# A start-up reorder, a contiguous sum of squares and a 64-byte shift of the stationary weights in a one-core encoder layer

## The chip, the cores and the metric

The kernel runs on one core of one Trainium2 chip. The metric is the device time of one execution in microseconds (us); the value before is the median of three runs. Engines are named as in the profile: PE is the matrix engine's multiplications and PEld its loading of stationary operands, DVE the vector engine, ACT the scalar engine, POOL the GpSimd engine, SP the engine that issues the transfers.

## The reference

One layer of a bidirectional encoder over 256 tokens of width 2048, all in float32:

```python
h = rmsnorm(x, norm_pre_mix)
u = h @ w_in                     # 2048 x 10240, cut into q, f_fwd, f_bwd, v, g
# 16 heads of 128: gated linear recurrence in both directions, summed over directions
o = rmsnorm(recurrence(silu(q), gates(f_fwd), gates(f_bwd), v), g_norm) * silu(g)
x = x + rmsnorm(o @ w_out, norm_post_mix)
h = rmsnorm(x, norm_pre_ffn)
gate, val = split(dwconv3(h @ ffn_w_in))     # 2048 x 11264
x = x + rmsnorm((silu(gate) * val) @ ffn_w_out, norm_post_ffn)   # 5632 x 2048
```

The root mean square of `x` is not divided out ahead of the first product. The kernel multiplies the unnormalised `x` (times the norm's weights) into `w_in` and scales the results by `rs1`, one number for each token, so that the first products need not wait for the sum of squares.

## The kernel before, in words

**Precision.** Float32 products are made of float32r parts. Every operand `a` is split into `hi` (ACT's rounded copy) and `lo = a - hi` (DVE). A product is then three products: hi with hi, hi with lo, lo with hi.

**Weights.** Each weight matrix is laid out in chunks of 512 output columns. A chunk is read in 1 MB transfers of `[128, 4, 512]` into one of three buffers `raw` (rows of 8192 bytes in each of the 128 partitions). `load(pieces)` can cut such a transfer into pieces, which makes the rows shorter in proportion. `prep` splits each half of a `raw` (a "sub", two steps `k` of 128 along the sum) into `hi` and `lo` in one of four buffers `wsp`: a cast on ACT (line 136) and a subtraction on DVE (line 137). The very first sub is split in two halves, so that its first half can be used early. `LOOK = 3` subs are prepared ahead; in the first chunk it is one.

**Two kinds of product.** `gemm` (lines 181, 184, 185) keeps activations stationary and streams 512 weight columns: three matmuls of 512 columns for each `k` and each of two token tiles. It serves the chunks of `v`, `g`, `w_out`, the first chunk of `ffn_w_in` and `ffn_w_out`. `gemm_t` (lines 221, 223) turns the product around: the weights are stationary (128 columns of `wsp`, called `w` in the code) and the activations are streamed. For each of 4 column tiles `n` and each `k` it makes a long matmul (`hi` stationary, activations `hi` and `lo` together, 512 columns, line 221) and a short one (`lo` stationary, activations `hi`, 256 columns, line 223). It serves the 12 chunks of `q`, `f` and `b` and 21 of the 22 chunks of `ffn_w_in`. A chunk of 16 steps `k` has 64 such pairs. In each sub all 8 long and all 8 short ones are run together, and a counter `turn` swaps which kind goes first from one sub to the next; in the last sub of a chunk the groups are two long, two short.

**Where the weights lie.** For chunks that `gemm_t` uses ("turned"), `hi` and `lo` lie a little into their buffers:

```python
at0 = [1088 * i + (OFF[i] if turned else 0) for i in range(2)]
```

`OFF` counts float32 elements. The stationary weights and the streamed activations then have addresses that differ by 4 x 48 = 192 bytes modulo 256. For `gemm` there is no such shift: streamed weights and stationary activations differ by a multiple of 256 bytes.

**The start.** SP issues the first transfers in the order of the code: parameters, two `k` of `x` (transposed, `xs`, `load_x`), two quarters of the first weights, two more `k` of `x`, the other two quarters, and so on. Meanwhile PE does 24 transposes of an identity (line 284). `split_x` makes `hi` (ACT, line 302) and `lo` (DVE, line 305) of two `k` of `x`, one call ahead of each sub of the first chunk.

**The sum of squares.** While the second chunk is multiplied, one step of a list (`soon`) is emitted after each sub: four steps `square_x` (ACT squares four `k` of `xs` in place, line 313; DVE sums them over `k` with a reduction whose innermost step runs across `k`, line 314) and a step `mean_x` (a last reduction, line 317; a matmul with a column of ones, line 320; the square root on POOL, line 230). Two steps later `spread` turns `rs1` into a row `r1` for all partitions.

**Order.** The program is built with `schedule_with_timeline_sim=True`: a planner with a model of the engines decides each engine's order, except where `keep_in_program_order` holds an instruction. Engines then run their own lists in that order and wait for each other by semaphores.

Of the kernel before, what the change touches and what calls it, by code (L numbers as in the profile page):

```python
# [11 lines left out]
F32 = mybir.dt.float32  # L12
# [3 lines left out]
ALU = mybir.AluOpType  # L16
AX = mybir.AxisListType

P = 128
T = 256  # L20
# [8 lines left out]
EPS = 1e-6  # L29
NLEV = 7  # L30
LOOK = 3
OFF = (48, 48)
WARM = 24

ORDER = [(s, g) for g in range(NG - 1) for s in "qfbgv"][:-1]
# [12 lines left out]
def encoder_layer(  # L48
# [13 lines left out]
    nc = tc.nc  # L62
    V, S, G = nc.vector, nc.scalar, nc.gpsimd

    def pool(stack, name, bufs=1, **kw):
        return stack.enter_context(tc.tile_pool(name=name, bufs=bufs, **kw))
# [10 lines left out]
    def stile(n, name):  # L77
        return small.tile([P, n], F32, name=name, tag=name)
# [24 lines left out]
    soon, later, extra = deque(), deque(), []  # L103

    def step():
        if soon or later:
            (soon or later).popleft()()

    def load(pieces=1):
        ci, s = subs[at["load"]]  # L110
        wd, c, _ = chunks[ci]
        raw = wraw.tile([P, 4, 512], F32, name="raw", tag="raw")
        src = wd[c, s // 2].rearrange("p (k n) -> p k n", n=512)
        w = 4 // pieces
        raws[ci, s // 2] = raw
        at["load"] += 2
        for i in range(pieces):
            nc.sync.dma_start(raw[:, w * i : w * i + w], src[:, w * i : w * i + w])
            yield

    def prep(upto):
        while at["prep"] < min(upto, len(subs)):
            i = at["prep"]
            if at["load"] <= i:
                list(load())
            ci, s = subs[i]
            src = raws[ci, s // 2][:, 2 * (s % 2) : 2 * (s % 2) + 2, :]
            pl, sfx = (extra[0], str(s)) if ci == C_UP - 1 and s >= 2 * chunks[ci][2] - 4 else (wspl, "")


            w = pl.tile([P, 2 * 1088], F32R, name="wsp", tag="wsp" + sfx)
            turned = ci < len(ORDER) and ORDER[ci][0] in "qfb" or C_UP < ci < C_UP + 2 * NJ
            at0 = [1088 * i + (OFF[i] if turned else 0) for i in range(2)]
            hi, lo = (w[:, o : o + 1024].rearrange("p (j n) -> p j n", n=512) for o in at0)
            for j in [slice(0, 1), slice(1, 2)] if i == 0 else [slice(0, 2)]:
                S.copy(hi[:, j], src[:, j])  # L136
                V.tensor_tensor(lo[:, j], src[:, j], hi[:, j].bitcast(F32), op=ALU.subtract)  # L137
            parts[ci, s] = (hi, lo)
            at["prep"] += 1
# [3 lines left out]
    def flush():  # L143
        while soon or later:
            step()
# [46 lines left out]
    def gemm_t(xx, need=None, pre=None):  # L192


        ci = at["chunk"]
        at["chunk"] += 1
        nsub = 2 * chunks[ci][2]
        base = subs.index((ci, 0))
        ps = [ps_g.tile([P, 2, T], F32, name="pg", tag="pg") for _ in range(4)]
        turn = [0]  # L200
        for s in range(nsub):
            if s == need:
                flush()
            prep(base + s + (LOOK if ci else 1))
            if pre:
                pre(s)
            hi, lo = parts[ci, s]

            tiles = [(n, 2 * s + j) for n in range(4) for j in range(2)]
            if ci == s == 0:
                tiles.sort(key=lambda nk: nk[1])
            for run in [tiles] if s < nsub - 1 else [tiles[i : i + 2] for i in range(0, 8, 2)]:
                long = turn[0] % 2 == 0
                for kind in (long, not long):
                    for n, k in run:
                        w = (hi if kind else lo)[:, k % 2, n * P : (n + 1) * P]
                        stop = s == nsub - 1 and kind != long and k == 2 * nsub - 1
                        if kind:  # L220
                            nc.tensor.matmul(ps[n], w, xx[:, k], start=(k == 0), stop=stop)  # L221
                        else:
                            nc.tensor.matmul(ps[n][:, 0, :], w, xx[:, k, 0, :], start=False, stop=stop)  # L223
                turn[0] += 1
            step()
        return ps

    def rsqrt_mean(dst, ss, n):
        V.tensor_scalar(dst, ss, 1.0 / n, EPS, op0=ALU.mult, op1=ALU.add)
        G.tensor_tensor(dst, dst, mneg[:, : dst.shape[1]], op=ALU.pow)  # L230

    def spread(rs, name):

        tp = ps_t.tile([P, 2, T], F32, name="tp", tag="tp")
        for m in range(2):
            a = rs[:, m : m + 1].broadcast_to([P, P])
            nc.tensor.matmul(tp[:, 0, m * P : (m + 1) * P], a, ident, start=True, stop=True)
        S.copy(name, tp[:, 0, :])
# [20 lines left out]
    spool = pool(sstack, "start", side="right")  # L259
    xs = spool.tile([P, KT, T], F32, name="xs")  # L260

    def load_x(a, b):
        nc.sync.dma_start(xs[:, a:b], xt_v[:, a:b])

    nc.sync.dma_start(prm[:, :C_CW], par[:, :C_CW])
    load_x(0, 2)
    first = load(4)
    next(first), next(first)
    load_x(2, 4)
    list(first)  # L270
    load_x(4, 8)
    list(load(2))
    load_x(8, 12)
    load_x(12, 16)
    make_identity(nc, ident)
    G.memset(mneg, -0.5)

# [22 lines left out]
    def split_x(k2):  # L300
        for k in (2 * k2, 2 * k2 + 1):
            S.activation(xx[:, k, 0, :], xs[:, k, :], AF.Copy, scale=prm[:, C_PRE + k : C_PRE + k + 1])
        for k in (2 * k2, 2 * k2 + 1):
            w1, hi = prm[:, C_PRE + k : C_PRE + k + 1], xx[:, k, 0, :].bitcast(F32)
            V.scalar_tensor_tensor(xx[:, k, 1, :], xs[:, k, :], w1, hi, op0=ALU.mult, op1=ALU.subtract)

    ss1, rs1 = spool.tile([P, 5, T], F32, name="ss1"), stile(2, "rs1")
    one = spool.tile([P, 1], F32, name="one")
    G.memset(one, 1.0)

    def square_x(q):
        k = slice(4 * q, 4 * q + 4)
        tc.keep_in_program_order(S.activation(xs[:, k], xs[:, k], AF.Square))
        V.tensor_reduce(ss1[:, q, :], xs[:, k].rearrange("p k t -> p t k"), axis=AX.X, op=ALU.add)

    def mean_x():
        V.tensor_reduce(ss1[:, 4, :], ss1[:, :4].rearrange("p q t -> p t q"), axis=AX.X, op=ALU.add)
        tp = ps_t.tile([P, 2, T], F32, name="tp", tag="tp")
        for m in range(2):
            nc.tensor.matmul(tp[:, 0, m : m + 1], ss1[:, 4, m * P : (m + 1) * P], one, start=True, stop=True)  # L320
        rsqrt_mean(rs1, tp[:, 0, :2], D)
        soon.extend([nop, lambda: spread(rs1, r1)])

    split_x(0)
    ps0 = gemm_t(xx, pre=lambda s: split_x(s + 1) if 2 * s + 2 < KT else None)
    soon.extend([lambda q=q: square_x(q) for q in range(4)] + [mean_x])
    ps1 = gemm_t(xx)
    load_rest()
    sstack.close()
# [28 lines left out]
    def do_q(g):  # L358
        ps = gemm_t(xx) if g else ps0
        qT = hp.tile([P, HG, T], F32, name="qT", tag="qT")  # L360
        each_token(ps, qT, r1)
        sg = nat.tile([P, HG, T], F32, name="qn", tag="qn")
        S.activation(sg, qT, AF.Sigmoid)
        V.tensor_tensor(qT, qT, sg, op=ALU.mult)
        st["q", g] = qT
# [419 lines left out]
```

## Time and profile before

| | |
|---|---|
| median of three runs | 1356.26 us (1356.21 to 1358.15) |
| profiled execution, its own time | 1357.99 us |
| span of its instructions | 1356.1 us |
| granted clock of the matrix engine, mean | 0.997 |
| PE busy | 1343.2 us, 99% |
| PEld busy | 1160.6 us, 86% |
| DVE busy | 956.4 us, 71% |
| ACT busy | 697.6 us, 51% |
| moved by the transfers | 248.90 MB, mean 184 GB/s |

The span runs from the first to the last instruction; the profiled execution's own time is 1.9 us longer, for what lies around it. An engine's busy time includes overlapped, modelled ends of pipelined matmuls, so the spacing of matmuls is better read from starts than from durations. The chain of waits lists, in order of time, the work that ended last and what released it.

### The profile page before, as it was taken

To read this page: it belongs to the slowest core of one execution; us is meant where nothing else is said; L and a number is where in the kernel's file an instruction comes from. 1 tells how busy PE (TensorE), PEld (TensorE's weight loads), DVE (VectorE), ACT (ScalarE), POOL (GpSimd) and SP (SyncE) were. 2 spreads that over 40 slices of the span, in tenths; PEclk is the share of its full clock that TensorE was granted. 3 is DMA by queue.
4 is the path that set the end of the run, shared out by engine and by line. 5 is a ranking of instruction groups with operands and counts; after the bars stand their busy time and mean duration, and the time that the engine had idled before them with its cause. 6 is when DMAs were issued, how large, how long until landed. Compare 5 with 4: busy or idle time off the path is not lost.

```text
span 1356.1 us, 18012 instructions
## 1 busy us (share of the span) xinstructions
PE 1343.2 (99%) x7244; PEld 1160.6 (86%) x7244; DVE 956.4 (71%) x1208; ACT 697.6 (51%) x964; POOL 12.5 (1%) x22
## 2 busy tenths in 40 slices
PE   8999999999999999999999999999999999999997
PEld 7888988898898888888888888888888888888886
DVE  6898768866996887567767777777768674444444
ACT  6555545455545545457655555555556554434342
POOL 0000000000000000000000000000000000000000
PEclk9999999999999999999999999999999999999999
DMA  8454445435444534673455555555555556555552
GB/s 307 167 186 168 145 172 181 163 135 187 174 142 167 190 135 156 248 254 115 169 208 186 187 189 187 200 186 201 186 187 187 189 187 240 191 186 191 202 197 93
DMA packets 36356, 248.90 MB, mean 184 GB/s; under 512 B 4144, under 2 KB 4400, under 8 KB 6832
## 3 DMA queue, kind: packets, MB, share of 16 engines
q1 hardware_dynamic: 36272, 247.75, 52.0%
q8 instruction: 57, 0.93, 0.3%
q14 instruction: 27, 0.22, 0.1%
HBM read 245.63 MB, written 2.10 MB: 183 GB/s over the span
## 4 chain that ended last, share of the span: by engine, by line
PE 97%; DVE 1%; DMA 0%; issue 0%; ACT 0%; SPq 0%; DVEq 0%; POOLq 0%; POOL 0%; ACTq 0%
PE pg L221 35%; PE pg L223 18%; PE pg L181 13%; PE pg L184 13%; PE pg L185 13%; PE sc L468 3%; PE sc L434 1%; PE sc L525 1%; PE sc L493 1%; PE sc L524 1%; DMA raw<-in_w_in 0%; DVE wsp L137 0%; PE tp L248 0%; PE tp L620 0%; ACT wsp L136 0%
## 5 line engine op out<-in xcount | busy, mean ns | idle before, releaser
L137 DVE TENSOR_TENSOR wsp<-raw,wsp 128x1024 fp32r<-128x1024 f32 (+1 forms) x457 | 555.0, 1221 | 337.8 <-ACT wsp L136 335.5
L136 ACT CAST wsp<-raw 128x1024 fp32r<-128x1024 f32 (+1 forms) x457 | 478.4, 1049 | 519.1 <-PE pg L185 224.8
L221 PE MATMUL pg<-hh,wsp 128*128 128x512 f32 x1344 | 332.2, 392 | 0.0
L221 PEld LDWEIGHTS pg<-hh,wsp 128*128 128x128 f32 x1344 | 241.9, 188 | 44.1
L221 PE MATMUL pg<-xx,wsp 128*128 128x512 f32 x768 | 195.3, 397 | 0.3 <-DVE qn L355 0.3
L223 PEld LDWEIGHTS pg<-hh,wsp 128*128 128x128 f32 x1344 | 177.5, 188 | 12.1
L223 PE MATMUL pg<-hh,wsp 128*128 128x256 f32 x1344 | 180.8, 278 | 0.0
L221 PEld LDWEIGHTS pg<-xx,wsp 128*128 128x128 f32 x768 | 139.0, 190 | 25.9 <-issue 0.7
L184 PE MATMUL pg<-wsp,gg 128*128 128x512 f32 x352 | 136.9, 389 | 0.0
L185 PE MATMUL pg<-wsp,gg 128*128 128x512 f32 x352 | 136.9, 389 | 0.0
L181 PE MATMUL pg<-wsp,gg 128*128 128x512 f32 x352 | 136.8, 389 | 0.0
L223 PEld LDWEIGHTS pg<-xx,wsp 128*128 128x128 f32 x768 | 103.4, 188 | 10.8 <-DVE wsp L137 3.4
L223 PE MATMUL pg<-xx,wsp 128*128 128x256 f32 x768 | 108.4, 280 | 3.0 <-DVE wsp L137 3.0
L184 PE MATMUL pg<-wsp,xx 128*128 128x512 f32 x256 | 100.1, 391 | 0.0
L185 PE MATMUL pg<-wsp,xx 128*128 128x512 f32 x256 | 100.0, 391 | 0.0
L181 PE MATMUL pg<-wsp,xx 128*128 128x512 f32 x256 | 97.2, 390 | 0.0
L185 PEld LDWEIGHTS pg<-wsp,gg 128*128 128x128 f32 x352 | 66.1, 188 | 13.8
L181 PEld LDWEIGHTS pg<-wsp,gg 128*128 128x128 f32 x352 | 66.1, 188 | 13.7
L184 PEld LDWEIGHTS pg<-wsp,gg 128*128 128x128 f32 x352 | 66.1, 188 | 13.6
L184 PEld LDWEIGHTS pg<-wsp,xx 128*128 128x128 f32 x256 | 48.1, 188 | 9.8
L181 PEld LDWEIGHTS pg<-wsp,xx 128*128 128x128 f32 x256 | 48.1, 188 | 9.8
L185 PEld LDWEIGHTS pg<-wsp,xx 128*128 128x128 f32 x256 | 48.1, 188 | 9.7
(137 smaller groups left out, 1178.0 us busy)
## 6 DMA issues: line engine op xcount, KB each, us to landing
raw<-in_w_up SPq DMA_DIRECT2D x88, 1024.0 KB, 4.9
raw<-in_w_in SPq DMA_DIRECT2D x78, 1024.0 KB, 4.9
raw<-in_w_dn SPq DMA_DIRECT2D x44, 1024.0 KB, 4.9
raw<-in_w_o SPq DMA_DIRECT2D x16, 1024.0 KB, 4.9
x<-in_x SPq DMA_DIRECT2D x1, 2048.0 KB, 7.7
wp<-in_post SPq DMA_DIRECT2D x2, 1024.0 KB, 6.2
out<-fw SPq DMA_DIRECT2D x8, 256.0 KB, 2.7
xs<-in_xt SPq DMA_DIRECT2D x3, 512.0 KB, 9.5
```

What stands on the lines that cost most here:

```text
L136: S.copy(hi[:, j], src[:, j])
L137: V.tensor_tensor(lo[:, j], src[:, j], hi[:, j].bitcast(F32), op=ALU.subtract)
L181: mm = nc.tensor.matmul(ps[m], a, hi[:, j, :], start=(k == 0), stop=False)
L184: nc.tensor.matmul(ps[m], a, lo[:, j, :], start=False, stop=False)
L185: nc.tensor.matmul(ps[m], b, hi[:, j, :], start=False, stop=(k == 2 * nsub - 1))
L221: nc.tensor.matmul(ps[n], w, xx[:, k], start=(k == 0), stop=stop)
L223: nc.tensor.matmul(ps[n][:, 0, :], w, xx[:, k, 0, :], start=False, stop=stop)
L434: nc.tensor.matmul(o, ones, a[:, i * 512 : i * 512 + 512], start=(j == 0), stop=(j == 1))
L468: nc.tensor.matmul(sc[:, j, :], kc[0][:, h, sl], r, start=True, stop=True)
L493: nc.tensor.matmul(sc[:, h, :], ks[:, d, h, s0 : s0 + P], qs[:, 1 - d, h, t0 : t0 + P], start=True, stop=True)
L524: nc.tensor.matmul(o[:, h, :], Sd[:, 2 * h + b, :], v[:, b, cs], start=True, stop=False)
L525: nc.tensor.matmul(o[:, h, :], So[1 - b][:, h, :], v[:, 1 - b, cs], start=False, stop=True)
```

## The change

Five edits in one:

1. `OFF` goes from 48 to 32 elements for both halves: stationary weights lie 128 in place of 192 bytes off the activations modulo 256.
2. In the first chunk the counter `turn` stays at zero, so that every sub there runs its long matmuls first.
3. The first 1 MB of weights comes in two pieces in place of four (rows of 4096 in place of 2048 bytes), the second 1 MB in one piece in place of two (8192 in place of 4096), the last half of `x` in one transfer in place of two (8192 in place of 4096).
4. The squares of `x` are summed by contiguous additions in place of reductions: three additions of 1024 elements in each partition, then one of 512 and one of 256.
5. The squares are done in two steps of `soon` in place of four, so `mean_x` comes two steps earlier.

```diff
-OFF = (48, 48)
+OFF = (32, 32)
...
-                turn[0] += 1
+                turn[0] += ci > 0
...
     nc.sync.dma_start(prm[:, :C_CW], par[:, :C_CW])
     load_x(0, 2)
-    first = load(4)
-    next(first), next(first)
+    first = load(2)
+    next(first)
     load_x(2, 4)
     list(first)
     load_x(4, 8)
-    list(load(2))
-    load_x(8, 12)
-    load_x(12, 16)
+    list(load())
+    load_x(8, 16)
...
-    ss1, rs1 = spool.tile([P, 5, T], F32, name="ss1"), stile(2, "rs1")
+    rs1 = stile(2, "rs1")
...
         tc.keep_in_program_order(S.activation(xs[:, k], xs[:, k], AF.Square))
-        V.tensor_reduce(ss1[:, q, :], xs[:, k].rearrange("p k t -> p t k"), axis=AX.X, op=ALU.add)
+        if q:
+            V.tensor_tensor(xs[:, :4], xs[:, :4], xs[:, k], op=ALU.add)

     def mean_x():
-        V.tensor_reduce(ss1[:, 4, :], ss1[:, :4].rearrange("p q t -> p t q"), axis=AX.X, op=ALU.add)
+        for n in (2, 1):
+            V.tensor_tensor(xs[:, :n], xs[:, :n], xs[:, n : 2 * n], op=ALU.add)
         tp = ps_t.tile([P, 2, T], F32, name="tp", tag="tp")
         for m in range(2):
-            nc.tensor.matmul(tp[:, 0, m : m + 1], ss1[:, 4, m * P : (m + 1) * P], one, start=True, stop=True)
+            nc.tensor.matmul(tp[:, 0, m : m + 1], xs[:, 0, m * P : (m + 1) * P], one, start=True, stop=True)
...
-    soon.extend([lambda q=q: square_x(q) for q in range(4)] + [mean_x])
+    soon.extend([lambda q=q: (square_x(q), square_x(q + 1)) for q in (0, 2)] + [mean_x])
```

## The prediction

> **What bounds the kernel now.** I read the page first: busy times and the chain that ended last.
>
> ```profile
> span 1356.1 us, 18012 instructions
> PE 1343.2 (99%) x7244; PEld 1160.6 (86%) x7244; DVE 956.4 (71%) x1208; ACT 697.6 (51%) x964; POOL 12.5 (1%) x22
> ...
> PE 97%; DVE 1%; DMA 0%; issue 0%; ACT 0%; SPq 0%; DVEq 0%; POOLq 0%; POOL 0%; ACTq 0%
> PE pg L221 35%; PE pg L223 18%; PE pg L181 13%; PE pg L184 13%; PE pg L185 13%; PE sc L468 3%; PE sc L434 1%; PE sc L525 1%; PE sc L493 1%; PE sc L524 1%; DMA raw<-in_w_in 0%; DVE wsp L137 0%; PE tp L248 0%; PE tp L620 0%; ACT wsp L136 0%
> ```
>
> PE carries 97% of the chain, so there are only two ways to move the time: shorten PE's few waits (3% of 1356 us hold them all, the tail at the end included), or change the spacing of the matmuls themselves. The turned products, lines 221 and 223, are 53% of the chain, the only ones whose addresses change.
>
> Then the spacing. First the chain inside one chunk of turned products (start, length, what; "x16" is 16 matmuls in a row), then the chain of the plain product (lines 181, 184, 185 in turn), last the durations (min/median/max in ns) of both kinds.
>
> ```profile
> 717.39 1.89 PE pg L223 x16
> 719.28 3.67 PE pg L221 x16
> ...
> 728.51 1.13 PE pg L223 x10
> ...
> 731.03 0.93 PE pg L221 x4
> ```
>
> ```profile
> 1109.95 0.23 PE pg L181
> ...
> 1126.27 0.23 PE pg L181
> ```
>
> ```profile
> L181 PE MATMUL pg<-wsp,gg x339: 389/389/389, 1109.8 to 1339.6; 128*128 128x512 f32 x170
> ...
> L221 PE MATMUL pg<-hh,wsp x1246: 388/392/397, 659.8 to 1090.0; 128*128 128x512 f32 x178
> ...
> L223 PE MATMUL pg<-hh,wsp x1240: 276/279/283, 661.9 to 1088.0; 128*128 128x256 f32 x178
> ```
>
> ```profile
> 719.12 3.83 PE L221 MATMUL pg<-hh,wsp 128*128 128x512 f32 x16
> ...
> 741.26 3.83 PE L221 MATMUL pg<-hh,wsp 128*128 128x512 f32 x16
> ```
>
> In the plain product 24 rounds of three take 1126.27 - 1109.95 = 16.32 us, 226.7 ns for 512 columns, and every one lasts 389 ns. In the turned one 512 columns take 3.67/16 = 229.4 ns, and durations scatter from 388 to 397. Its 256-column matmuls take 1.89/16 = 118 ns in some runs and 1.13/10 = 113 ns in others; 113 is half of 226.7. So something adds to the turned matmuls what the plain ones don't pay, now and then. A whole turned chunk of 64 pairs repeats every 741.26 - 719.12 = 22.14 us, 345.9 ns for a pair; at 226.7 + 113.3 it would be 340.0. The excess, 5.9 ns on each of 33 x 64 = 2112 pairs, is 12.5 us in all.
>
> Last the start, the only place with a large wait: PE, ACT and the clock there.
>
> ```profile
> 6.44 2.35 PE L221 MATMUL pg<-xx,wsp 128*128 128x512 f32 x8
> 8.63 1.07 PE L223 MATMUL pg<-xx,wsp 128*128 128x256 f32 x8
> 12.26 1.21 PE L223 MATMUL pg<-xx,wsp 128*128 128x256 f32 x8 [2.56 <-DVE wsp L137]
> ```
>
> ```profile
> 6.91 0.62 ACT L136 CAST wsp<-raw 128x512 fp32r<-128x512 f32 x1 [0.66 <-DMA raw<-in_w_in]
> ...
> 9.90 1.04 ACT L136 CAST wsp<-raw 128x1024 fp32r<-128x1024 f32 x1 [1.42 <-DMA raw<-in_w_in]
> ...
> 12.89 1.05 ACT L136 CAST wsp<-raw 128x1024 fp32r<-128x1024 f32 x1
> 14.15 1.04 ACT L136 CAST wsp<-raw 128x1024 fp32r<-128x1024 f32 x1 [0.21 <-DMA raw<-in_w_in]
> ```
>
> ```profile
> 10.98 1.24 DVE wsp L137
> 12.21 0.04 issue
> 12.26 1.21 PE pg L223 x8
> 13.47 5.27 PE pg L221 x16
> 18.73 1.30 PE pg L223 x11
> ```
>
> ```profile
> 5.00:6.00 1.00, 1.00 (x7) 1.00 (x6) 0.99 (x4) 0.64 (x2) 0.00 (x0) 1.00 0.86 264
> ...
> 14.00:15.00 1.00, 1.00 (x3) 0.73 (x3) 1.00 (x1) 0.85 (x1) 0.00 (x0) 0.50 1.08 447
> ```
>
> PE has the first sub done at 9.70, then stands still for 2.56 us: the second half of the first 1 MB lands at 9.9, ACT casts, and since this sub starts with short matmuls, DVE's subtraction has to end too (12.2). Afterwards the granted clock is 0.50 for a while (seventh number of the 14 to 15 us row), and 16 long matmuls take 5.27 us in place of 3.67: 1.60 us more.
>
> **The parts and their sum.** The profiled execution took 1357.99 us, 1.73 us above the median. The slow-clock stretch costs 1.6 us, nearly the same, so I take it that the runs at 1356.2 had no such stretch, and that 1358.15 had it. The sum is made against the profiled time and then set against the median.
>
> [...]
>
> *Start: pieces and turn (edits 2 and 3).* One piece of 4096-byte rows stands for two of 2048, so ACT's first cast can't start before what was the second piece is there: 6.91 at the latest. It casts 512 columns in 0.62, so PE starts at about 7.5, 1.0 us later than now, and needs (3.67 + 1.89)/2 = 2.78 for a sub: first sub done at 10.3. The third and fourth quarter land at 9.9 at the latest; 9.90 + 1.04 is 10.95, and with long matmuls first PE waits only for the cast: 0.65 us in place of 2.56. DVE's 1.24 then hides behind the 8 long matmuls (1.83). The second sub ends at 13.7. But the next 1 MB is now one transfer, and its end landed at 14.15 in the present order, where the first half was ready for ACT at 12.89. PE's third sub therefore starts at 14.15 + 1.04 = 15.2 and ends at 18.0: a new wait of 1.5 us. In the profile the third sub's long ones end at 18.74 and half of the 16 short ones (0.94) at 19.7. So the start gains 1.7 us against the profiled execution and 0.1 us against one without the slow clock. Longer rows should bring the landings forward: the first microseconds moved 264 GB/s (2048-byte rows), the stretch at 14 us 447 GB/s (4096 and longer); but that is also the time since the start, so I bound the gain by 0 and by 1 us (14.15 to 13.15) and take 0.3. Splits of `x` for the third sub precede its cast on ACT as now; the last half of `x` in one transfer is needed in the fifth sub, not before 20 us. SP's queue gets four issues fewer ahead of the later loads, which wait for free buffers anyway. Start: -0.4 us against the median (0.1 + 0.3), -2.0 against the profiled execution; ends -1.1 and +1.5 (the new wait triggers a slow stretch in its turn).
>
> *Squares (edits 4 and 5).* The costs on DVE, by form, in the first 60 us (count, busy, mean ns):
>
> ```profile
> L137 DVE TENSOR_TENSOR wsp<-raw,wsp 128x1024 fp32r<-128x1024 f32 x19 | 22.9, 1222 | 11.0 <-ACT wsp L136 11.0
> L314 DVE TENSOR_REDUCE ss<-xs 128x256 f32<-128x1024 f32 x4 | 8.1, 2029 | 0.0
> ...
> L317 DVE TENSOR_REDUCE ss<-ss 128x256 f32<-128x1024 f32 x1 | 2.0, 2014 | 0.0
> L355 DVE TENSOR_TENSOR qT<-pg,qT 128x256 f32<-128x256 f32 x4 | 1.5, 402 | 0.0
> L137 DVE TENSOR_TENSOR wsp<-raw,wsp 128x512 fp32r<-128x512 f32 x2 | 1.4, 692 | 0.9 <-ACT wsp L136 0.9
> ```
>
> Removed: 4 x 2.03 + 2.01 = 10.1 us. Added: 3 x 1.22 + 0.69 + 0.40 = 4.8 us. DVE has 5.4 us less to do, and `rs1` comes two subs, 5.5 us, earlier. Nearly all of it is hidden, since PE hardly waits for DVE there. What PE does wait is:
>
> ```profile
> 61.10 1.08 PE L221 MATMUL pg<-xx,wsp 128*128 128x512 f32 x4
> 62.48 0.71 PE L221 MATMUL pg<-xx,wsp 128*128 128x512 f32 x2 [0.29 <-DVE qn L355]
> ...
> 69.92 1.10 PE L223 MATMUL pg<-xx,wsp 128*128 128x256 f32 x8
> 71.50 0.74 PE L223 MATMUL pg<-xx,wsp 128*128 128x256 f32 x4 [0.47 <-DVE wsp L137]
> ```
>
> The first is a queue of DVE work held up until `r1` was there, the second a subtraction behind the gates of `f`. By the starts of the rows, 4 long ones from 61.10 at 229 ns end their turn at 62.02, 0.46 us ahead of the next, and 8 short ones from 69.92 at 118 ns at 70.86, 0.64 ahead: at most 1.1 us together. I take 0.8 off; ends 0 and -1.1. Two squares in one step put 2.1 us on ACT in a row ahead of a cast, but three subs (8.3 us of PE) are prepared ahead; without that cover it would cost those 2.1 us.
>
> *The shift (edit 1).* It adds no instruction. No row shows 128 bytes. At 0 bytes the plain products show no excess, at 192 the turned ones 5.9 ns a pair. Lower end: the excess goes, -12.5 us. Upper end: all short ones at 118, as in the slower runs above, and all long ones as in the slowest group of four, 0.93/4 = 232.5: 350.5 ns a pair, 4.6 more than now, +9.7 us. [...] The 113 ns runs, which the present shift reaches already, are nearest to what a good shift gives, so I lean to a gain and take a little over a fifth of the way to the lower end, 1.3 ns a pair: -2.8 us. It is the weakest term.
>
> Sum: -0.4 - 0.8 - 2.8 = -4.0 against the median, 1352.3 us (against the profiled 1357.99: -2.0 - 0.8 - 2.8 = -5.6, 1352.4).
>
> **The rivals.**
>
> *The shift does nothing* (the excess is not a matter of addresses). For it: stationary loads last 187 to 188 ns in both kinds of product:
>
> ```profile
> L221 PEld LDWEIGHTS pg<-hh,wsp x1246: 187/188/189, 659.8 to 1090.0; 128*128 128x128 f32 x178
> ```
>
> Against it: the same matmul form with the same load is even in one place and scattered in the other. Then -0.4 - 0.8 = -1.2: 1355.1 us.
>
> [...]
>
> *The shift hurts* (the other side). 128 bytes is the farthest from the plain products' 0 that there is modulo 256. If the excess grows with that distance, long matmuls go towards 232.5 and all short ones to 118; halfway to the upper end is +4.8, with the rest 1359.9 us. It decides from 1.9 ns more a pair on (347.8 ns): 1.9 x 2.112 = 3.9 us outweighs the 1.2 and 2.7 more.
>
> *The shift removes it all*: -12.5 - 1.2 = 1342.6 us.
>
> **How the numbers follow.** A change of 0.2%, 2.7 us, is about what a measurement of this kernel can tell. A part of the excess goes (likeliest, 1348 to 1353.5): 0.46. All or nearly all goes (1342 to 1348): 0.11. Both are faster: 0.57. No effect of the shift, with the start between its ends (1353.6 to 1358.9): 0.26, same. The shift hurts (above 1359): 0.17, slower. The range leaves out half of the second case and a third of the last: 1344 to 1361.
>
> **What would show it.** Line 221's durations at a constant 389 and a turned chunk every 21.8 us would show the whole excess gone; 22.05 us the likeliest case; more than 22.2 us the third rival. The start is right if PE's wait after the first sub is under 1 us, a new one of 1 to 1.5 us stands ahead of the third sub and ends with the landing of the 1 MB transfer, and no row has a clock of 0.50. It is wrong if that new wait is over 2.5 us. The squares are right if DVE's additions on `xs` last 1.2 us and the waits at 62 and 71 us are gone. The prediction fails above all if a turned chunk's period moves otherwise than by 0.0 to 0.2 us.

## The result, and the profile after

The changed kernel takes 1365.17 us (median of 5 runs, 1364.87 to 1366.36), the kernel before 1356.26 us (5 runs): a ratio of 1.0063, 95% interval 1.0052 to 1.0074. It is 8.9 us slower. The forecast was 1352.3 us with a range up to 1361.0, so time and direction were both missed. Two single executions of later runs, 3492.09 us with the activations moved and 2111.77 us at 224 bytes (the second with a mean granted clock of 0.595), lie far above all others of the same kernels and are left out of the times given for these kernels.

First the page of the changed kernel: PE is as much the bound as before, and the group of line 221 on `hh` has a mean of 395 ns, where it had 392 (last line).

```profile
span 1363.1 us, 18001 instructions
...
PE 98%; DMA 1%; issue 0%; SPq 0%; DVE 0%; ACT 0%; DVEq 0%; POOLq 0%; POOL 0%
...
L221 PE MATMUL pg<-hh,wsp 128*128 128x512 f32 x1344 | 336.8, 395 | 0.0
```

```profile
L221 PE MATMUL pg<-hh,wsp 128*128 128x512 f32 x1344 | 332.2, 392 | 0.0
```

The chain in the same kind of chunk as shown of before (start, length, what):

```profile
718.33 1.90 PE pg L223 x16
720.23 3.71 PE pg L221 x16
...
729.57 1.19 PE pg L223 x10
...
740.82 1.90 PE pg L223 x16
```

And the durations there (min/median/max in ns), turned products first, then the plain last product:

```profile
L221 PE MATMUL pg<-hh,wsp x1226: 390/393/405, 659.6 to 1089.1; 128*128 128x512 f32 x176
...
L223 PE MATMUL pg<-hh,wsp x1222: 274/281/288, 661.9 to 1089.9; 128*128 128x256 f32 x175
...
L181 PE MATMUL pg<-wsp,gg x334: 389/389/390, 1118.3 to 1344.7; 128*128 128x512 f32 x167
```

A turned chunk repeats every 740.82 - 718.33 = 22.49 us where it was 22.14. If all 33 chunks lost as much, that is 0.35 x 33 = 11.6 us. The run of ten short matmuls, 1.13 us before, takes 1.19: the quick runs at 113 ns are gone. The plain product has not moved. By this count 11.6 us were lost in the turned chunks, and 2.7 us won elsewhere. The start shows where part of that is:

```profile
7.70 2.12 PE L221 MATMUL pg<-xx,wsp 128*128 128x512 f32 x8 [1.00 <-ACT wsp L136]
...
10.62 2.02 PE L221 MATMUL pg<-xx,wsp 128*128 128x512 f32 x8
...
12.47 1.10 PE L223 MATMUL pg<-xx,wsp 128*128 128x256 f32 x8
12.74 2.00 ACT L136 CAST wsp<-raw 128x1024 fp32r<-128x1024 f32 x2 [0.79 <-DMA raw<-in_w_in]
...
13.83 2.12 PE L221 MATMUL pg<-xx,wsp 128*128 128x512 f32 x8 [0.26 <-ACT wsp L136]
```

PE starts 1.3 us later, but then no longer stands still after the first sub, and waits 0.26 us ahead of the third. The same two microseconds of both kernels (last number: GB/s), before first:

```profile
6.00:7.00 1.00, 1.00 (x5) 0.92 (x4) 0.69 (x1) 0.34 (x2) 0.00 (x0) 1.00 0.87 289
7.00:8.00 1.00, 1.00 (x6) 0.75 (x5) 0.43 (x1) 0.96 (x3) 0.00 (x0) 1.00 0.92 317
```

```profile
6.00:7.00 1.00, 0.70 (x4) 0.38 (x2) 0.00 (x0) 0.00 (x0) 0.00 (x0) 1.00 0.99 358
7.00:8.00 1.00, 0.30 (x1) 0.30 (x2) 0.32 (x1) 0.97 (x2) 0.00 (x0) 1.00 1.06 410
```

SP's issue of the second 1 MB of weights, which the third sub needs, in two pieces before and in one after (start, length):

```profile
4.48 1.34 SPq L118 DMA_DIRECT2D raw<-in_w_in  x2
```

```profile
3.53 0.69 SPq L118 DMA_DIRECT2D raw<-in_w_in  x1
```

The additions that replace the reductions, by form, in the first 60 us:

```profile
L314 DVE TENSOR_TENSOR xs<-xs 128x1024 f32<-128x1024 f32 x3 | 3.7, 1223 | 0.7 <-ACT xs L312 0.7
...
L318 DVE TENSOR_TENSOR xs<-xs 128x512 f32<-128x512 f32 x1 | 0.7, 693 | 0.0
L318 DVE TENSOR_TENSOR xs<-xs 128x256 f32<-128x256 f32 x1 | 0.4, 425 | 0.0
```

### The profile page after: what moved, and what is told of

The parts are those of the page before. It is cut to its first block, busy times and chain, and to the rows that moved or that the text cites. A ratio compares the mean times of both kernels' runs of the same rounds, so it can differ in the third digit from the quotient of the medians.

```text
span 1363.1 us, 18001 instructions
## 1 busy us (share of the span) xinstructions
PE 1352.4 (99%) x7244; PEld 1164.9 (85%) x7244; DVE 952.5 (70%) x1208; ACT 697.1 (51%) x964; POOL 14.4 (1%) x22
## 4 chain that ended last, share of the span: by engine, by line
PE 98%; DMA 1%; issue 0%; SPq 0%; DVE 0%; ACT 0%; DVEq 0%; POOLq 0%; POOL 0%
PE pg L221 36%; PE pg L223 18%; PE pg L185 13%; PE pg L184 13%; PE pg L181 13%; PE sc L469 3%; DMA raw<-in_w_in 1%; PE sc L435 1%; PE sc L494 1%; PE sc L525 1%; PE sc L526 1%; PE tp L248 0%; PE tp L621 0%; DVE fw L722 0%; SPq L263 0%
## 5 line engine op out<-in xcount | busy, mean ns | idle before, releaser
L221 PE MATMUL pg<-hh,wsp 128*128 128x512 f32 x1344 | 336.8, 395 | 0.0
L223 PE MATMUL pg<-hh,wsp 128*128 128x256 f32 x1344 | 183.8, 281 | 0.0
```

## The experiments

Two theories stood at the outset: the shift alone costs the time, or the order of matmuls and the planner's other choices do. All times below are medians; the kernel before had medians of 1356.19 to 1356.55 us beside them.

**The shift put back, the rest kept.**

```diff
-OFF = (32, 32)
+OFF = (48, 48)
```

> The changed kernel with the shift alone put back from 128 to 192 bytes. Theory A (the shift costs it all): a turned chunk goes from 22.50 us back to 22.14, 33 x 0.36 = 11.8 us less than 1365.2, so 1353.4 us, and that is faster than before by 2.8 us, what the other edits bring. Rival B (the spacing comes from the new order of the matmuls or the planner's other choices, not from the addresses): chunks stay at 22.50 and the time at 1365.

Measured: 1353.87 us (10 runs), ratio to before 0.9977, interval 0.9968 to 0.9987. Its chain has the rows of before again:

```profile
715.27 3.67 PE pg L221 x16
718.94 1.88 PE pg L223 x16
...
724.50 1.13 PE pg L223 x10
```

It is 11.3 us below the whole change. This version is the fastest of all that ran.

**The shift alone, in the kernel before.**

```diff
-OFF = (48, 48)
+OFF = (32, 32)
```

> The kernel before with the shift alone set to 128 bytes. Theory A: turned chunks at 22.50 us, 1356.3 + 11.8 = 1368.1 us, slower than the whole change. Rival B: 1356.3 and chunks at 22.14.

Measured: 1367.82 us, ratio 1.0082, interval 1.0067 to 1.0097: 11.4 us for the shift by itself. Its timeline (start, length) repeats after 744.69 - 722.20 = 22.49 us:

```profile
722.20 3.88 PE L221 MATMUL pg<-hh,wsp 128*128 128x512 f32 x16
...
744.69 3.88 PE L221 MATMUL pg<-hh,wsp 128*128 128x512 f32 x16
```

Both runs say theory A, and the costs add up: -2.6 from the rest and +11.4 from the shift make 8.8, against 8.9 measured for both.

**Other distances.** In the changed kernel, `OFF = (0, 0)` and `OFF = (16, 16)`:

> The changed kernel with no shift (0 bytes modulo 256). If the plain products' 389 ns comes from their 0 bytes (theory A1, distance from 0 decides), turned chunks fall to 21.76 us and the time to 1353.4 - 33 x 0.38 = 1340.9 us. If what decides is where the stationary load stands against the stream in this order of matmuls, long and short ones mixed (theory A2), 0 need not be better than 192: 22.1 to 22.8 us a chunk, 1353 to 1375 us.

> The changed kernel with a shift of 16 elements, 64 bytes. By distance from 0 modulo 256 (A1), 64 is the same as 192: chunks at 22.14 us, 1353.4 us. By the direction of the shift (A2, ahead of the stream and behind it differ) it is another value, 22.2 to 22.8 us, 1355 to 1375 us.

Measured: 1358.99 us at 0 bytes (ratio 1.0021, interval 1.0012 to 1.0030) and 1356.34 at 64 bytes (0.9998, 0.9988 to 1.0007). The chain at 0 bytes, then at 64:

```profile
715.32 1.91 PE pg L223 x16
717.24 3.65 PE pg L221 x16
...
737.63 1.91 PE pg L223 x16
```

```profile
715.33 1.82 PE pg L223 x16
717.15 3.73 PE pg L221 x16
...
737.52 1.82 PE pg L223 x16
```

A chunk takes 22.31 us at 0 and 22.19 at 64 bytes. Distance from 0 (A1) falls: 64 and 192 bytes differ, and 0 is not free. At 0 the long matmuls are the quickest, 3.65/16 = 228 ns, and the short ones slow, 119; at 64 the short ones are the quickest in runs of sixteen, 114, and the long ones slow, 233; at 192 the long ones take 229 and the short ones 113 in the run of ten and 118 in runs of sixteen; at 128 both are slow, 232 and 119 in the rows of the whole change above.

**Hi and lo apart.** That suggested 0 for the hi weights and 64 for the lo weights, `OFF = (0, 16)`, and as a control `OFF = (16, 0)`:

> The changed kernel with the shift of the hi weights 0 bytes and of the lo weights 64 bytes. In the runs with one shift for both, groups of 16 long matmuls were quickest at 0 bytes and the short ones at 64 bytes (113 to 114 ns). Theory C (each kind's spacing is set by the shift of its own weights, since the load that runs beside a long matmul is mostly the next hi one): long 226.7 to 229 and short 113.3 to 114.5, a pair at 340 to 343.5 against 345.9 at 192 bytes, 2112 x 2.4 to 5.9 ns = 5 to 12.5 us below 1353.9: 1341 to 1349 us. Rival D (the two kinds can't be set apart, the phase that one leaves decides the next): near the mean of the 0 and 64 byte runs, 1357.7 us.

> The opposite: hi 64 bytes, lo 0. Theory C: long at 232.4, short at 119.3, a pair at 351.7, 5.8 ns over 345.9: 1353.9 + 12.2 = 1366 us. Rival D: 1357.7.

Measured: 1355.81 us (ratio 0.9991, 0.9982 to 1.0001) and 1365.69 us (1.0064, 1.0049 to 1.0079). The first run's chain, then the second's:

```profile
715.97 3.65 PE pg L221 x16
719.63 1.89 PE pg L223 x16
```

```profile
718.88 1.90 PE pg L223 x16
720.77 3.74 PE pg L221 x16
```

The bad pair is as bad as theory C had it, the good pair isn't as good. The long matmuls go by the hi shift, as theory C has it: 228 ns at 0 and 233 to 234 at 64 bytes, whatever the lo shift. The short ones don't go by their own shift alone: the same lo shift of 64 bytes that gave 114 ns with hi weights at 64 gives 118 with hi weights at 0. The mean that rival D forecast, 1357.7, is missed too, by 1.9 and 8.0 us. So the two settings can't be chosen apart; what ties them together isn't shown.

**Is it modulo 256, and is it the distance?** `OFF = (64, 64)` in the changed kernel; and the shift left at 128 bytes, with the activations moved down by 64:

```diff
-    xx = acts.tile([P, KT, 2, T], F32R, name="xx", tag="xx")
+    xx = acts.tile([P, KT * 2 * T + 16], F32R, name="xx", tag="xx")
+    xx = xx[:, : KT * 2 * T].rearrange("p (k i t) -> p k i t", i=2, t=T)
```

(and the same for `hh`, which takes the same place; the tiles that lie beside them on that side, `oo` among them, move along).

> The changed kernel with a shift of 64 elements, 256 bytes. If only the distance modulo 256 bytes counts, the same as no shift: 1359.0 us and chunks at 22.3 us. If it is the distance itself, or modulo 512 or more, another time: 1353 to 1366.

> The changed kernel (weights shifted by 128 bytes) with the normed activations and what lies beside them moved down by 64 bytes: weights stay where they are, and stand 192 bytes off the activations again. Theory E (what counts is the distance between stationary load and stream): turned chunks back from 22.50 to 22.14 us, -11.8 us; and the plain products on these activations (13 chunks of 96 matmuls), whose stationary load now stands 192 bytes off their stream in place of 0, go from 226.7 to about 229.5 ns, 1248 x 2.8 = +3.5 us: 1365.2 - 11.8 + 3.5 = 1356.9 us, while the last product, whose activations are not moved, stays at 389 ns. Rival F (the weights' own place in the store counts): 1365.2, chunks at 22.50.

Measured: 1358.90 us at 256 bytes, the time of 0 (1358.99), with the same rows:

```profile
715.52 1.91 PE pg L223 x16
717.43 3.65 PE pg L221 x16
```

And 1356.54 us with the activations moved, where 1356.9 was expected by theory E and 1365.2 by rival F. In that run, durations of line 221, of the plain product on the moved `xx` and of the plain one on `gg`, which is not moved (each with min/median/max), and then the plain product on `xx` in the kernel before:

```profile
L221 PE MATMUL pg<-hh,wsp x1244: 388/392/397, 659.7 to 1089.4; 128*128 128x512 f32 x178
...
L185 PE MATMUL pg<-wsp,xx x196: 387/394/488, 90.1 to 479.9; 128*128 128x512 f32 x196
...
L185 PE MATMUL pg<-wsp,gg x339: 389/389/389, 1109.6 to 1339.5; 128*128 128x512 f32 x170
```

```profile
L185 PE MATMUL pg<-wsp,xx x199: 388/389/492, 90.0 to 478.3; 128*128 128x512 f32 x199
```

The turned products have their old durations (388/392/397) and their old period (739.97 - 717.83 = 22.14 us in the timeline) although the weights stayed in place, and the plain ones on the moved `xx` are slowed on two of their three lines: medians of 394 on line 185 and 392 on line 184, both 389 before, while line 181 has 388. So it is the distance between the load's and the stream's addresses that counts, and it counts with weights or with activations as the stationary operand.

**Between the steps.** Shifts of 32, 96, 160 and 224 bytes, `OFF = (8, 8)`, `(24, 24)`, `(40, 40)`, `(56, 56)`:

> The changed kernel with a shift of 8 elements, 32 bytes. Steps of 64 bytes (the same piece as 0): 1359 us, 22.31 us a chunk. Smooth curve between 0 (1359.0) and 64 bytes (1356.3): 1357.7.

> 24 elements, 96 bytes. Steps: as 64 bytes, 1356.3 us, 22.2 us a chunk. Smooth between 64 (1356.3) and 128 bytes (1365.2): 1360.8.

> 40 elements, 160 bytes. Steps: as 128 bytes, 1365.2 us, 22.50 us a chunk. Smooth between 128 (1365.2) and 192 bytes (1353.9): 1359.5.

> 56 elements, 224 bytes. Steps: as 192 bytes, 1353.9 us, 22.14 us a chunk. Smooth between 192 (1353.9) and 256 bytes (1358.9): 1356.4. Either way not better than 192 bytes; a time under 1353 would be a better place than any tried.

Measured: 1365.50, 1366.21, 1368.82 and 1362.28 us. Neither theory holds: each is slower than both its neighbours, if at 96 bytes by only 1 us over 128, which the intervals of the two don't tell apart. The four distances that are no multiple of 64 bytes cost 8 to 15 us over 192 bytes.

| distance, bytes | 0 | 32 | 64 | 96 | 128 | 160 | 192 | 224 | 256 |
|---|---|---|---|---|---|---|---|---|---|
| time, us | 1359.0 | 1365.5 | 1356.3 | 1366.2 | 1365.2 | 1368.8 | 1353.9 | 1362.3 | 1358.9 |

**The other edits one by one**, each in the kernel before, with the shift at 192: the start's two edits; the squares; the transfers alone; the order alone.

```diff
 # the order alone
-                turn[0] += 1
+                turn[0] += ci > 0
```

> The kernel before with the edits of the start alone (longer rows and long matmuls first in the first chunk); shift and sums of squares as before. Theory: the landings come forward, the third sub's weights land at 12.7 us, PE's wait after the first sub is gone and no slow clock stretch follows; with the squares worth at most 1.1 us, the start has 1.5 to 2.5 of the 2.6 us that shift 192 gained: 1353.9 to 1354.9 us. Rival (the squares bring it): 1356.0 or more.

> The kernel before with the sums of squares alone changed (contiguous additions, two steps). From the start's 1.2 to 1.3 us and the 2.6 of start and squares together, 1.3 us remain: 1355.1, with PE's waits at 62 and 71 us gone and the slow stretch at the start still there in some executions. The prediction's own number was 0.8: 1355.6. If the squares do nothing: 1356.4.

> The kernel before with the transfers of the start alone changed (two pieces, then whole ones), the order of long and short matmuls as before. The second sub's weights land before 9 us, it waits for DVE at 11.3 in place of 12.3, the third sub's for the 1 MB landing at 12.7 to 13.2: about the time of both edits of the start, 1355.3 us. If the order matters more than the landing: 1356 or more.

> The kernel before with long matmuls first in the first chunk, transfers as before. Landing at 9.9, cast until 10.95, no wait for DVE: PE's wait falls from 2.56 to 1.3 us, and the third sub is ready at 13.9: also 1355.1 to 1355.5 us, with no slow stretch. If the landing matters more than the order: 1356 or more.

Measured: the start 1355.25 us (ratio 0.9988, 0.9979 to 0.9997), the squares 1354.76 (0.9988, 0.9979 to 0.9998), the transfers alone 1355.35 (0.9990, 0.9981 to 1.0000), the order alone 1356.05 (0.9994, 0.9985 to 1.0004). Against the medians of the kernel before that were taken with them (1356.55 and 1356.35), start and squares are worth 1.3 and 1.6 us; together they made 2.6 with the shift at 192, which their sum of 2.9 fits. PE in the start with the transfers alone, then with the order alone:

```profile
7.80 2.11 PE L221 MATMUL pg<-xx,wsp 128*128 128x512 f32 x8 [1.01 <-ACT wsp L136]
...
11.44 1.21 PE L223 MATMUL pg<-xx,wsp 128*128 128x256 f32 x8 [0.58 <-DVE wsp L137]
```

```profile
11.22 2.12 PE L221 MATMUL pg<-xx,wsp 128*128 128x512 f32 x8 [1.73 <-ACT wsp L136]
...
20.15 2.12 PE L221 MATMUL pg<-xx,wsp 128*128 128x512 f32 x8 [0.27 <-ACT wsp L136]
```

The transfers alone bring 1.0 of the 1.3 us that both edits bring, but its interval reaches to no change, so how the gain divides between the two isn't shown. The order alone can't be told from no change: it takes DVE out of the wait, but 1.73 us of it remain, ended by ACT's cast.

## Why the prediction was wrong

*The shift* is the step that failed. It was put at -2.8 us and measured +11.3 and +11.4: wrong sign, and beyond the upper end of +9.7 that the text had for it. Three things were wrong in it.

- The lean to a gain rested on the 113 ns runs being "nearest to what a good shift gives". Quick short runs don't hang on the shift of their own weights alone, as the 114 and 118 ns at one lo shift show, and their presence said nothing on what another shift gives.
- The upper end took today's slowest rows for the worst that could be. At 128 bytes the mean pair is 22.49/64 = 351.4 ns, over the 350.5 supposed: long matmuls and short ones are slow together throughout the chunk. At 160 bytes it is worse still, 22.61/64 = 353.3 ns. The bound was made from rows of one distance, and a bound for another distance doesn't follow from them.
- The third rival had the right sign, with a chance of 0.17 and a price of 4.8 us at its middle. Its reason (128 bytes as the farthest from 0) doesn't hold, as 0 is worse than 64 and 192. Why 128 is the worst of the four stays open.

That the excess is a matter of addresses was argued from 389 throughout against 388 to 397. That is now shown, by moving the activations in place of the weights (1356.54 against 1365.17 us). With the same instructions, the distance of load and stream changed the spacing of matmuls, to 22.49 us a chunk at 128 bytes and 22.61 at 160 (742.93 - 720.32 in the timeline), from 22.14 at 192.

*The start* had the right places but the landing wrong. The text took 14.15 less 0.3 us for the 1 MB of the third sub; it had landed at 12.7. The text put the four issues fewer on SP at nothing; but with them the 1 MB was issued at 3.53 us, where its two pieces had been issued from 4.48 to 5.82. The transfers also moved 358 and 410 GB/s in two microseconds in which they had moved 289 and 317. Row length and number of issues changed together, so what each did to the landing isn't shown. PE's wait after the first sub went to nothing (0.65 was forecast), the new one ahead of the third sub to 0.26 us (1.2 to 1.5 forecast). The term was -0.4 with an end of -1.1; alone it measured -1.3, in an interval from -2.8 to -0.4.

*The slow stretch.* The text held that the pause of 2.56 us drops the clock in some executions only and costs 1.6 us then. Of 25 runs of the kernel before in one session, 15 had a mean clock of 0.998 or more and 1355.65 to 1356.95 us, 10 had 0.997 and 1356.93 to 1357.93. With start and squares changed and the shift at 192, all 10 runs had 0.998 or more. That fits, but it isn't shown. The mean doesn't say where the clock was low, and 0.997 also came in two of five runs of the changed kernel, whose profile has no pause after the first sub, in two of ten with the start's edits alone, and in four of ten at 0 bytes. Nor is the pause the same in each execution. With the start as before it lasted 1.96 us in the profile of the squares alone (below), and there the 16 long matmuls behind it took 16.42 - 12.69 = 3.73 us, where they took 5.27 in the profile of before.

```profile
11.64 1.21 PE L223 MATMUL pg<-xx,wsp 128*128 128x256 f32 x8 [1.96 <-DVE wsp L137]
12.69 3.89 PE L221 MATMUL pg<-xx,wsp 128*128 128x512 f32 x16
16.42 2.04 PE L223 MATMUL pg<-xx,wsp 128*128 128x256 f32 x16
```

So the slow stretch stood behind the pause of 2.56 us and not behind the one of 1.96; what decides it isn't shown.

*The squares* were put at -0.8 with an end of -1.1 and measured -1.6, with an interval that reaches from -2.8 to -0.3. DVE's rows are as forecast (1.22, 0.69, 0.43 against 0.40), and the waits at 62 and 71 us are gone from PE's timeline. What lies beyond the 1.1 us of these waits can't be told from the noise of the measurement.

## What to carry to other kernels

Where PE is the bound at 97%, look at the spacing of equal matmuls before anything else: a scatter of durations where another place of the same kernel has a constant can weigh more than the waits, here 11.4 us for a move of 64 bytes against 2.6 us for start and squares together. The distance between the addresses of stationary load and stream, modulo 256 bytes (256 took 1358.9 us and 0 took 1359.0), is a setting that has to be measured: try the four multiples of 64 bytes first (the distances between them were no better here than their neighbours), and try them again whenever an operand moves (64 bytes of the activations were worth 8.6 us here). The estimate from rows of one setting gave neither the sign nor a bound for another (-2.8 us, +9.7 at most, against +11.3 measured), so such an edit is tested alone and not bundled with others that gain.

## What the runs showed of the hardware

In this kernel the spacing of the float32r matmuls, each with a stationary load of its own, goes by the distance between the addresses of load and stream: 1353.9, 1356.3, 1359.0 and 1365.2 us for the same instructions at distances of 192, 64, 0 and 128 bytes, and 1362.3 to 1368.8 at the four distances tried between these. A distance of 256 bytes gives the time of 0 again (1358.9). Of 0 and 64 bytes, 512 columns are quicker at 0 (228 against 233 ns) and 256 columns at 64 (114 against 119), and the spacing of the short ones also hangs on the shift of the hi weights (114 or 118 ns at one lo shift). No run looked at single accesses: what load and stream do to each other, and why the distances come in this order, stays open.
